# A hybrid two-layer backbone whose instruction order is set by the framework's timeline model

## The chip, the cores and the metric

The kernel runs on one core of a Trainium2 chip. The metric is the device time of one execution in microseconds (us), as a median of several executions. The core has five engines that run their own instruction streams in program order: TensorE (PE, matrix products), VectorE (DVE), ScalarE (ACT), GpSimd (POOL) and SyncE (SP, whose instructions here only issue DMA transfers). An engine that meets an instruction whose input isn't there yet waits, and everything behind that instruction on the same engine waits with it.

## What is computed

The reference is a backbone of two layers over 1024 latent tokens and 256 context tokens, 1024 wide, in float32.

```python
def hybrid_layer(x_lat, x_ctx, mod_lat, mod_ctx, p, layer_idx, need_ctx):
    sh1, sc1, g1, sh2, sc2, g2 = jnp.split(mod_lat[:, None, :], 6, axis=-1)
    ...
    hl = rms_norm(x_lat, p['norm1_g']) * (1.0 + sc1) + sh1
    ...
    zl = split_cols(hl @ p['w_in'])
    ...
    s5 = s5_mixer(zc[0], zl[0], p, need_ctx)
    ml = mlstm_mixer(zc[1:6], zl[1:6], p, need_ctx)
    da = diff_attention_mixer(zc[6:9], zl[6:9], p, layer_idx, need_ctx)
    gl = gla_mixer(zc[9:14], zl[9:14], p, need_ctx)
    mix_l = jnp.concatenate([s5[1], ml[1], da[1], gl[1]], axis=-1) @ p['w_out']
    x_lat = x_lat + g1 * mix_l
    hl2 = rms_norm(x_lat, p['norm2_g']) * (1.0 + sc2) + sh2
    x_lat = x_lat + g2 * sq_relu_mlp(hl2, p['mlp_w1'], p['mlp_w2'])
```

The context tokens go through the same layer with their own modulation, except that the second layer needs no context output (`need_ctx` is false there). The four mixers are a state space model (S5), an mLSTM, differential attention and gated linear attention (GLA).

## The kernel before

**Arithmetic.** Every large product is done as three products of split operands (a high and a low part of each side), at the helper's lines L1124, L1125 and L1126. So three matmuls stand for one. A weight block comes from memory into a tile `raw` (L1112, on SP's queue, three buffers that the modulation's weights `adaw`, L1159, share), ACT casts it to `whi` (L1115), and DVE forms the rest `wlo` (L1116).

**Stages of a layer.** The input projection writes PSUM tiles `zp`; ACT copies each to `zst` (L1261), and a DMA stores it. The S5 mixer runs beside it: PE multiplies the input blocks (`s5pv`, L350), ACT, POOL and DVE run the state recurrence (`s5V`, `s5W`, `s5Z`, `s5X`), and PE reads the state out (`s5py`, L308 and L313). `da_prep` rotates the attention's queries and keys and stores them (`da_st`, L447). GLA follows (`glpl` L1014, `glpo` L1059 and L1064, and the mean square for its norm, `glms` L1072). Then comes differential attention: scores `daps` (L486), their copy with a running maximum on DVE (`das`, L487), exponentials on ACT (L498), the combination of the two maps on DVE (L506), transposes `dapt` (L527), the product with the values `dapo` (L518), and a norm (`dams` L552). The mLSTM runs beside attention: a convolution and an activation prepare its queries and keys on DVE and ACT (tiles `mlcy`, `mlqT`, `mlkT`, L722 to L734), then PE transposes (`mlpt` L756) and updates states (`mlpu` L788). The first half of the output projection (`wop`, needing only S5 and GLA) is also put beside attention; its second half follows. Then come a norm (`np`, `npm`) and the MLP (`m1p`, `m2p`). In layer 0's MLP the S5 tables of layer 1 (`s5_prep`) and the modulation (`ada`) are computed beside the products.

**What sets the order.** The Python code issues the instructions in one sequence. Generators are interleaved by helpers; three such places matter here:

```python
        beside(both(s5_mix(...), 2, dap, 1), rest, 1300)
        ...
        beside(gla, rest, 1400)
        ...
        beside((1 for _ in both(da, 1, ml, 0.25)), po, 0.12)
```

Here `rest` are the steps of the input projection, `po` those of the first half of the output projection, and the number says how much filler goes beside one step. On top of this sequence the tile framework has a scheduler: it keeps a model of the machine, goes through the instructions, and sets for each engine the order in which they are written to that engine's stream. So the order on an engine need not be that of the code. Data dependencies and the reuse of buffers are kept by semaphores in any order.

## Time and profile before

| | |
|---|---|
| median of 3 executions | 3724.48 us (3724.34 to 3726.04) |
| the profiled execution | 3719.97 us, span 3718.2 us |
| PE busy | 3435.5 us, 92% of the span |
| PE's weight loads (PEld) busy | 2725.4 us, 73% |
| DVE busy | 2228.8 us, 60% |
| ACT busy | 1309.4 us, 35% |
| POOL busy | 450.7 us, 12% |
| mean granted TensorE clock | 0.952 |

The span is that of one profiled execution, from its first instruction to its last. Busy time counts an engine's own instructions; successive matmuls overlap in PE's pipeline, so a busy PE isn't one that works at its peak. The granted clock is a share of the full 2.4 GHz; the rows know two levels, 0.5 (1.2 GHz) and 1.0 (2.4 GHz), and a value between them in a stretch is a mean.

### The profile page before, as it was taken

The page shows a single profiled execution, that of the slowest core. Times are in us where ns is not written, and L with a number is a line of the kernel's source. Part 1 is how long each engine was busy: PE and PEld are TensorE (multiplying, and loading weights), DVE is VectorE, ACT ScalarE, POOL GpSimd, SP SyncE. Part 2 cuts the span into 40 slices and gives each one's busy share as a digit, 9 for nine tenths or more (in the row PEclk, how much of TensorE's full clock was granted, in tenths as well). Part 3 has the DMA queues.
Part 4 walks back from the last instruction along what each step waited for, and adds up shares of the span by engine and source line. Part 5 has one row for each costly group of instructions (what it writes and reads, how often), then busy time and mean ns, then how long its engine had stood idle before and what let it go on. Part 6 is the DMA issues. An engine that isn't in the chain of part 4 may idle for free. (4 is left out here: it accounts for less than half of the span.)

```text
span 3718.2 us, 53487 instructions
## 1 busy us (share of the span) xinstructions
PE 3435.5 (92%) x20338; PEld 2725.4 (73%) x20338; DVE 2228.8 (60%) x5455; ACT 1309.4 (35%) x2457; POOL 450.7 (12%) x520
## 2 busy tenths in 40 slices
PE   6989998798889999999999798988889899999998
PEld 3867767576658888888888476867677578888885
DVE  9654685877659855455544637486788543333334
ACT  4223434766542121212121522435676431222222
POOL 2121221222100000000000123120222000000000
PEclk8979999898899999999999998999889899999999
DMA  5665324655461221222111265314653611111112
GB/s 216 230 205 154 129 77 133 214 183 166 141 208 57 90 82 69 81 74 86 61 39 42 102 201 161 120 57 143 213 167 104 205 46 51 46 51 46 52 47 78
DMA packets 233959, 430.23 MB, mean 116 GB/s; under 512 B 47415, under 2 KB 135911, under 8 KB 233447
## 3 DMA queue, kind: packets, MB, share of 16 engines
q1 hardware_dynamic: 192806, 381.03, 31.2%
q10 hardware_dynamic: 35520, 30.52, 2.6%
q0 software_dynamic: 5376, 15.28, 1.2%
q8 instruction: 160, 2.62, 0.3%
q14 instruction: 97, 0.79, 0.1%
HBM read 316.88 MB, written 109.86 MB: 115 GB/s over the span
## 5 line engine op out<-in xcount | busy, mean ns | idle before, releaser
L1562 DVE SCALAR_TENSOR_TENSOR X<-m2p,mods,X 128x256 f32<-128x256 f32 (+1 forms) x512 | 345.7, 683 | 345.1 <-PE m2p L1126 344.6
L1115 ACT CAST whi<-raw 128x1024 fp32r<-128x1024 f32 x182 | 191.1, 1050 | 919.8 <-PE m2p L1125 638.0
L1124 PE MATMUL m2p<-hidhi,whi 128*128 128x512 f32 (+1 forms) x1280 | 473.8, 372 | 3.5 <-DVE X L1562 2.8
L1124 PE MATMUL m1p<-h2hi,whi 128*128 128x512 f32 (+1 forms) x1280 | 474.3, 371 | 0.2 <-ACT h2hi L1209 0.2
L1125 PE MATMUL m1p<-h2lo,whi 128*128 128x512 f32 (+1 forms) x1280 | 473.6, 370 | 0.0
L1125 PE MATMUL m2p<-hidlo,whi 128*128 128x512 f32 (+1 forms) x1280 | 473.1, 370 | 0.0
L1126 PE MATMUL m2p<-hidhi,wlo 128*128 128x512 f32 (+1 forms) x1280 | 472.2, 370 | 0.8 <-DVE wlo L1116 0.8
L1126 PE MATMUL m1p<-h2hi,wlo 128*128 128x512 f32 (+1 forms) x1280 | 472.6, 370 | 0.0
L1116 DVE TENSOR_TENSOR wlo<-raw,whi 128x1024 fp32r<-128x1024 f32 x182 | 224.7, 1235 | 313.2 <-ACT whi L1115 301.2
L1124 PEld LDWEIGHTS m2p<-hidhi,whi 128*128 128x128 f32 x1280 | 241.6, 189 | 59.6 <-issue 8.6
L1124 PEld LDWEIGHTS m1p<-h2hi,whi 128*128 128x128 f32 x1280 | 243.1, 190 | 46.2 <-ACT whi L1115 4.2
L1126 PEld LDWEIGHTS m2p<-hidhi,wlo 128*128 128x128 f32 x1280 | 241.2, 188 | 46.4 <-issue 3.4
L1125 PEld LDWEIGHTS m1p<-h2lo,whi 128*128 128x128 f32 x1280 | 243.4, 190 | 40.8 <-DVE h2lo L1210 0.8
L1126 PEld LDWEIGHTS m1p<-h2hi,wlo 128*128 128x128 f32 x1280 | 243.2, 190 | 40.3 <-issue 0.4
L1125 PEld LDWEIGHTS m2p<-hidlo,whi 128*128 128x128 f32 x1280 | 241.6, 189 | 42.0 <-issue 2.2
L1124 PE MATMUL zp<-hhi,whi 128*128 128x512 f32 (+1 forms) x664 | 254.2, 383 | 11.6 <-ACT zst L1237 9.6
L487 DVE TENSOR_SCALAR_CACHE_REDUCE das<-daps 128x512 f32<-128x512 f32 (+1 forms) x400 | 226.0, 589 | 58.4 <-PE daps L486 55.0
L1125 PE MATMUL zp<-hlo,whi 128*128 128x512 f32 (+1 forms) x664 | 251.2, 378 | 5.6 <-DVE hlo L1205 5.2
L1126 PE MATMUL zp<-hhi,wlo 128*128 128x512 f32 (+1 forms) x664 | 249.5, 376 | 0.0
L1576 DVE TENSOR_TENSOR rl<-rl,m1p 128x256 f32<-128x256 f32 (+1 forms) x160 | 100.8, 631 | 177.1 <-ACT rl L1575 177.1
L498 ACT ACTIVATE das<-das,danm 128x1280 f32<-128x1280 f32 x128 | 174.3, 1362 | 42.7 <-DVE danm L496 42.3
L486 PE MATMUL daps<-daqk,daqk 128*128 128x512 f32 (+1 forms) x400 | 153.3, 447 | 38.0 <-DVE das L487 36.6
(460 smaller groups left out, 6671.3 us busy)
## 6 DMA issues: line engine op xcount, KB each, us to landing
raw<-w SPq DMA_DIRECT2D x136, 512.0 KB
adaw<-ada_w SPq DMA_DIRECT2D x96, 512.0 KB
whl<-wsp SPq DMA_DIRECT2D x80, 512.0 KB
wsp<-whl SPq DMA_DIRECT2D x32, 512.0 KB
raw<-wz SPq DMA_DIRECT2D x30, 512.0 KB
daqk<-da_st SPq DMA_DIRECT2D x24, 640.0 KB
mlE<-ml_rows SPq DMA_DIRECT2D x16, 640.0 KB
xn<-xo SPq DMA_DIRECT2D x72, 128.0 KB
```

The lines of the kernel that those rows point to most:

```text
L486: pe.matmul(p[:, 0:b - a], Q[m][:, 128 * qt:128 * qt + 128], K[m][:, a:b], start=True, stop=True)
L487: v.tensor_scalar(s[:, a:b], p[:, 0:b - a], -1.0, None, op0=ALU.mult, op1=ALU.min, accum_out=pm[:, i:i + 1])
L498: act.activation(s[:, :k1], s[:, :k1], AF.Exp, bias=nm[:, 0:1], scale=-1.0, accum_out=sm[m])
L1115: nc.scalar.copy(hi, raw)
L1116: nc.vector.tensor_tensor(lo, raw, hi.bitcast(F32), op=ALU.subtract)
L1124: pe.matmul(out, ah, bh, start=i == 0, stop=False)
L1125: pe.matmul(out, ah, bl, start=False, stop=False)
L1126: pe.matmul(out, al, bh, start=False, stop=i == n - 1)
L1562: nc.vector.scalar_tensor_tensor(X[b][:, m], p[:, :n], mod(l, 5, s)[:, m:m + 1], X[b][:, m], op0=ALU.mult, op1=ALU.add)
L1576: nc.vector.tensor_tensor(rl[:, :n], rl[:, :n], p[:, :n], op=ALU.mult)
```

## The change

```diff
-    with tile.TileContext(nc) as tc:
+    with tile.TileContext(nc, schedule_with_timeline_sim=True) as tc:
         tile_hybrid_backbone(tc, io, out)
```

The framework's scheduler now goes by a timeline model of the machine in place of its default model. The instructions are the same in kind and number, with the same tiles and pools; what differs is their order on each engine, and with it the semaphore waits that go along (3,160 semaphore instructions where there were 3,118).

**S5 and the projection in layer 0, on PE.** In the rows of an engine's order a number behind a tile's name is its buffer, and xN stands for N equal instructions in a row. Before, where the first S5 groups of layer 0 begin, PE had:

```order
L1126 MATMUL zp<-hhi_377,wlo 128x512
L350 MATMUL s5pv<-U,s5mi 64x160 x16
L308 MATMUL s5py<-U,s5toep 128x160
L313 MATMUL s5py<-s5X,s5mo 128x160 x4
L308 MATMUL s5py<-U,s5toep 128x160
L313 MATMUL s5py<-s5X,s5mo 128x160 x4
L350 MATMUL s5pv<-U,s5mi 64x160 x8
L1162 MATMUL adap<-adaw,cst 32x512 x4
L1169 MATMUL adap_2272<-selada,adar 128x2 x4
```

Now it has first

```order
L350 MATMUL s5pv<-U,s5mi 64x160 x8
L308 MATMUL s5py<-U,s5toep 128x160 x2
L350 MATMUL s5pv<-U,s5mi 64x160 x8
L313 MATMUL s5py<-s5X,s5mo 128x160 x4
L1124 MATMUL zp<-hhi_379,whi 128x512
L1125 MATMUL zp<-hlo_380,whi 128x512
L1126 MATMUL zp<-hhi_379,wlo 128x512
```

and, behind 16 more rows of `zp`,

```order
L313 MATMUL s5py<-s5X,s5mo 128x160 x4
L1125 MATMUL zp<-hlo_380,whi 128x512
L1126 MATMUL zp<-hhi_379,wlo 128x512
L1124 MATMUL zp<-hhi_379,whi 128x512
L1125 MATMUL zp<-hlo_380,whi 128x512
L1126 MATMUL zp<-hhi_379,wlo 128x512
L350 MATMUL s5pv<-U,s5mi 64x160 x8
L1169 MATMUL adap_2272<-selada,adar 128x2 x4
L1124 MATMUL zp<-hhi_375,whi 128x256
L1125 MATMUL zp<-hlo_376,whi 128x256
L308 MATMUL s5py<-U,s5toep 128x160
L1126 MATMUL zp<-hhi_375,wlo 128x256
```

Products of the projection now stand between the groups of S5, where before 47 instructions of S5 and the modulation stood next to each other. On SP the load of projection weights (`raw`, L1112) that stood behind the first four rows of S5's table loads (`s5tbl`, L346), and the load of the value weights `wn` that stood behind eight such rows, now stand ahead of the first.

**The end of GLA and the start of attention in layer 0, on PE.** Before, the last product of GLA stood 267 instructions ahead of these rows, with `zp` alone between:

```order
L1126 MATMUL zp<-whi,hlo_380 128x256
L672 MATMUL mlpt<-ident,ig 128x104
L673 MATMUL mlpt<-ident,mlbb 128x104
L681 MATMUL mlpt<-mlam,mle 128x40
L756 MATMUL mlpt<-ident,mlkT 128x128 x10
L788 MATMUL mlpu<-mlvx,mlkw 64x65
L486 MATMUL daps<-daqk_6076,daqk_6078 128x256
L486 MATMUL daps<-daqk_6072,daqk_6074 128x256
L486 MATMUL daps<-daqk_6076,daqk_6078 128x256 x2
L486 MATMUL daps<-daqk_6072,daqk_6074 128x256
L486 MATMUL daps<-daqk_6076,daqk_6078 128x512 x2
L486 MATMUL daps<-daqk_6072,daqk_6074 128x512
L1124 MATMUL wop<-mh,whl 128x256
```

Now the products of GLA are spread among those of the projection, 12 to 37 `zp` between two groups, and the end is this, with `zp` ahead of it:

```order
L1126 MATMUL zp<-whi,hlo_380 128x256
L1072 MATMUL glms<-glsq,bones 128x512
L1014 MATMUL glpl<-glqd_4176,glkt 64x256 x4
L1014 MATMUL glpl<-glqd_4177,glkt 64x256 x4
L1014 MATMUL glpl<-glqd_4176,glkt 64x256 x4
L486 MATMUL daps<-daqk_6076,daqk_6078 128x256
L1014 MATMUL glpl<-glqd_4177,glkt 64x256 x4
L1014 MATMUL glpl<-glqd_4176,glk 64x256 x4
L1059 MATMUL glpo<-glqd_4177,glS_3586 64x2x64 x4
L1059 MATMUL glpo<-glqd_4176,glS_3587 64x2x64 x4
L1064 MATMUL glpo<-glA,glv 64x64 x8
L1059 MATMUL glpo<-glqd_4177,glS_3586 64x2x64 x4
```

followed, behind one more row of `glpo`, by

```order
L1064 MATMUL glpo<-glA,glv 64x64 x8
L1072 MATMUL glms<-glsq,bones 128x256 x2
L486 MATMUL daps<-daqk_6076,daqk_6078 128x256
L486 MATMUL daps<-daqk_6072,daqk_6074 128x256
L486 MATMUL daps<-daqk_6076,daqk_6078 128x256
L486 MATMUL daps<-daqk_6072,daqk_6074 128x256
L486 MATMUL daps<-daqk_6076,daqk_6078 128x512 x2
L486 MATMUL daps<-daqk_6072,daqk_6074 128x256
L486 MATMUL daps<-daqk_6072,daqk_6074 128x512
L1124 MATMUL wop<-mh,whl 128x256
L1125 MATMUL wop<-ml,whl 128x256
```

The last block of GLA (the context tokens') now comes behind the projection with nothing beside it, and attention starts at once behind it. The mLSTM's transposes `mlpt`, which stood ahead of the first scores, come among the attention's rows, 47 to 214 instructions behind the first eight scores in a row, and the first `mlpu` stands 242 instructions behind them, where it stood just ahead. On DVE the mLSTM's convolution (L723, L734) stood ahead of the first `das`, and now stands 52 to 140 rows behind it. In layer 1, which has no context block, GLA is spread in the same way, 19 `zp` stand between its last `glpo` and its last `glms`, and the mLSTM's preparation stays ahead of the first `das`.

**Elsewhere.** In attention the `wop` rows come in whole groups of 12, and in layer 0 they reach to the last 40 instructions ahead of the last `dams`, where before the last 200 had none. Behind the last `dams` the `wop` of the second half follow at once in both. In the MLPs `m1p` and `m2p` keep their order; layer 1's S5 tables, which were spread to the end of layer 0's MLP, are now done by its middle.

## Rows read from the trace of the kernel before

**Rows 1.** The page's first part: busy time, share of the span, instructions.

```profile
PE 3435.5 (92%) x20338; PEld 2725.4 (73%) x20338; DVE 2228.8 (60%) x5455; ACT 1309.4 (35%) x2457; POOL 450.7 (12%) x520
```

**Rows 2.** Engines' busy time, TensorE clock, DMA by stretch: four long stretches.

```profile
core 0: us, PE busy (x) PEld busy (x) DVE busy (x) ACT busy (x) POOL busy (x), PEclk, DMA share, GB/s
68.00:656.00 588.00, 530.49 (x3770) 419.94 (x3767) 378.57 (x835) 216.07 (x417) 120.58 (x153) 0.92 0.49 154
656.00:995.00 339.00, 299.25 (x2290) 235.59 (x2290) 271.39 (x919) 220.05 (x496) 78.54 (x76) 0.92 0.53 172
2155.00:2597.00 442.00, 394.75 (x2847) 320.45 (x2845) 278.44 (x512) 161.61 (x291) 102.04 (x112) 0.95 0.42 131
2597.00:2931.00 334.00, 290.71 (x2121) 225.51 (x2120) 257.88 (x811) 213.21 (x445) 74.04 (x62) 0.88 0.53 170
```

**Rows 3.** The same view, by stage.

```profile
214.00:387.00 173.00, 157.38 (x883) 122.95 (x878) 95.98 (x216) 52.34 (x114) 41.28 (x61) 0.85 0.56 178
387.00:450.00 63.00, 58.97 (x692) 48.80 (x691) 44.91 (x84) 29.14 (x54) 14.58 (x8) 1.00 0.33 116
450.00:565.00 115.00, 102.70 (x759) 69.74 (x758) 95.36 (x163) 46.84 (x85) 31.60 (x24) 0.97 0.21 71
565.00:605.00 40.00, 37.11 (x321) 32.35 (x321) 20.61 (x46) 12.28 (x30) 7.14 (x8) 1.00 0.21 69
605.00:638.00 33.00, 32.01 (x263) 31.41 (x262) 19.77 (x45) 17.86 (x24) 2.74 (x18) 1.00 0.63 151
638.00:656.00 18.00, 3.59 (x19) 2.63 (x18) 13.92 (x18) 15.20 (x29) 0.00 (x0) 0.58 0.97 323
995.00:1118.00 123.00, 98.51 (x443) 62.64 (x443) 61.16 (x101) 50.05 (x90) 5.07 (x7) 0.92 0.60 202
1118.00:2054.00 936.00, 932.74 (x5039) 780.07 (x5038) 548.22 (x1491) 182.78 (x318) 35.65 (x69) 0.99 0.20 68
2155.00:2350.00 195.00, 172.22 (x1002) 140.99 (x1001) 105.49 (x217) 50.37 (x105) 55.47 (x65) 0.93 0.55 167
2350.00:2413.00 63.00, 61.85 (x673) 51.67 (x672) 37.20 (x67) 30.79 (x55) 9.60 (x6) 1.00 0.31 109
2413.00:2530.00 117.00, 103.84 (x717) 75.73 (x718) 99.51 (x152) 44.78 (x76) 31.80 (x22) 0.96 0.17 58
2530.00:2597.00 67.00, 56.85 (x462) 52.07 (x458) 36.24 (x78) 35.68 (x56) 5.16 (x19) 0.92 0.56 171
```

**Rows 4.** PE's waits, S5 stage of layer 0, 212 to 390 us.

```profile
PE s5py L313 <- DVE s5X L374: 4.3, 1, 4.3
PE s5py L308 <- DVE s5Y L316: 3.6, 4, 1.8
```

**Rows 5.** Loads of raw weights on SP's queue, 200 to 300 us.

```profile
L1112 SPq DMA_DIRECT2D raw<-wn x2: 424/427/430, 282.3 to 283.4; - x2
L1112 SPq DMA_DIRECT2D raw<-wz x1: 431/431/431, 233.8 to 233.8; - x1
```

**Rows 6.** PE's waits, GLA stage of layer 0, 390 to 605 us.

```profile
PE glpl L1014 <- DVE glqd L1007: 7.9, 10, 2.3
PE glms L1072 <- ACT glsq L1070: 4.0, 3, 2.0
```

**Rows 7.** PE's waits, first attention head, layer 0, 636:757.

```profile
PE mlpu L788 <- issue: 11.0, 1, 11.0
PE daps L486 <- DVE das L487: 9.4, 8, 6.4
```

**Rows 8.** PE's waits, S5 stage of layer 1, 2155:2350.

```profile
PE s5py L313 <- DVE s5X L374: 14.2, 4, 7.0
```

**Rows 9.** The same view, instructions on tile mlcy alone: DVE, ACT, clock, DMA.

```profile
605.00:656.00 51.00, 21.90 (x24) 5.82 (x4) 0.85 0.75 212
```

**Rows 10.** PE's waits between attention and MLP, layer 0, 995:1118.

```profile
PE wop L1124 <- ACT mh L1444: 9.0, 3, 7.4
```

## The prediction

> **What bounds the kernel now.** I read the page's busy shares first. PE is busy for 92% of the span and DVE for 60% [rows 1], so PE sets the time, but a busy PE includes matmuls at half clock and matmuls that overlap. I therefore read busy time and clock by stretch, and for each stretch took what PE loses: wall time less busy time times granted clock. That is the time in which PE either had nothing to do or did it at 1.2 GHz. A better order can give back this time and no other, since the products themselves stay.
>
> The layer 0 MLP shows a stretch without such loss: 936 us of wall, 932.74 busy at 0.99, so 936 - 923 = 13 us lost [rows 3]. The reader should see that a quarter of the span lies there, and that next to nothing is to be had in it; layer 1's MLP is the same work for fewer tokens. The four mixer stretches are different [rows 2]: 588 - 530.49 x 0.92 = 100 us lost in the projection with S5 and GLA of layer 0, 339 - 275 = 64 in its attention, 442 - 375 = 67 in layer 1's projection with S5 and GLA, 334 - 256 = 78 in layer 1's attention. The change works on these 309 us.
>
> By stage [rows 3] the loss of the projection parts is this. S5 of layer 0 (214 to 387 us): 173 - 157.38 x 0.85 = 39. GLA of layer 0 (387 to 605): 4 + 15.4 + 2.9 = 22. The projection's tail (605 to 638) loses 1, so the products alone fill PE. The step into attention (638 to 656) loses 18 - 3.59 x 0.58 = 16. S5 of layer 1 (2155 to 2350): 195 - 160 = 35. GLA of layer 1 and the step into its attention (2350 to 2597): 1 + 17.3 + 14.7 = 33.
>
> The waits tell why. In S5, PE stands at the read-out for DVE's states, 4.3 us and 3.6 us in layer 0 [rows 4] and 14.2 us in layer 1 [rows 8], and nothing of the projection stands in between on PE to fill this. Loads are one reason: between 200 and 300 us SP issued only three loads of projection weights, the first at 233.8 us and the others at 282.3 to 283.4 us [rows 5]. The named waits make only a fifth of the 39 us; the rest is the clock, 157.38 x 0.15 = 24 us, which fell while PE had only small products with pauses. In GLA, PE stands for `glqd` ten times, 7.9 us, and for the norm's squares, 4.0 us [rows 6]. So both stages have the form of short stalls in a chain over DVE and ACT, with 33 us of pure projection work [rows 3] left behind them in which nothing stalls.
>
> **The change, part by part.** The sum is made against the profiled execution's own time, 3719.97 us, which is 4.5 us under the median of 3724.48.
>
> *S5 with the projection, both layers.* The order now puts `zp` products between the S5 groups. At the first place of layer 0 the run of S5 and modulation without a `zp` shrinks from 47 instructions to 22, and the later groups have one to nineteen `zp` between them. Nothing is added: the products come out of the tail, where they were not covering anything. 25 of 47 is 53%, and later groups are covered better, so I take 60% of the loss: 0.6 x 39 = 23 in layer 0 and 0.6 x 35 = 21 in layer 1. The bounds: only the waits named in the rows, 8 and 14, or the whole, 39 and 35.
>
> *GLA with the projection, both layers.* With 12 to 37 `zp` between two groups, the waits for `glqd` have cover. DVE is the next engine: it worked 95.36 of 115 us in the dense part (450 to 565), but over 387 to 638 it has 44.91 + 95.36 + 20.61 + 19.77 = 181 us of 251 [rows 3], so spreading GLA over the tail leaves DVE room. The same 60% gives 0.6 x 22 = 13 and 0.6 x 33 = 20. The bounds: 8 and 8 (the named `glqd` waits, for layer 1 taken as in layer 0), or 22 and 33.
>
> *The step into attention, layer 0.* Gone is the stall at the first `mlpu`, 11.0 us, and the longest at `daps`, 6.4 us [rows 7]; with the clock this was 16 us plus 6, or 22. In its place stands the context block of GLA with no `zp` beside it. The trace has no such uncovered block; the nearest rows are the longest waits of a covered one, 2.3 us for a group of `glpl` and 2.0 for `glms` [rows 6]. Five groups and two norms make 5 x 2.3 + 2 x 2 = 15.5 us, and the first `wop` must wait for its operand `mh`, whose longest wait elsewhere was 7.4 us [rows 10]: 23 us. So the one stall takes the place of the other and I put 0, with bounds of -10 (the chain overlaps the first scores) and +20 (both stalls stay, as `mlpu` only moves).
>
> *The mLSTM's preparation, layer 0.* It lay under the projection's tail and the step behind it; now it stands behind the first `das`. On DVE the convolution's tile alone takes 21.9 us, on ACT 5.8 [rows 9]. In attention DVE has 271.39 of 339 us [rows 2], 68 us free, so it may cost nothing; if DVE sets attention's pace it costs 21.9. DVE is four fifths full there, and long instructions in front of a `das` hold up `daps` on PE: I take +10. Queued behind them on DVE are the score copies, and for these PE's scores wait, with `wop` groups between as cover. The Trainium skill (SBUF — State Buffer, section "SBUF: two separate sides") says that a DVE operation with two SBUF inputs and a GpSimd operation that reads SBUF shut each other out for whole instructions. The convolution has two such inputs; POOL was busy for 2.74 us of the tail but for 78.54 of 339 us in attention, so by this rule an estimate is 0.23 x 21.9 = 5 us more, and the sum would be 5 us higher. No run here shows it yet, and the sum goes without it.
>
> *Attention's fillers.* Whole groups of `wop` up to the end give the transposes cover, but spread what there is; the second half of the output projection must still wait for the last head. The stretch behind attention already loses 123 - 98.51 x 0.92 = 32 us, of which 9.0 are waits for `mh` [rows 10, 3]. With no `wop` left over I put +4 for each layer's end, and nothing for the cover in the middle. Bounds: -10 and +15 in all for each layer.
>
> *The MLPs.* Their products keep their order, and the S5 tables of layer 1 run on DVE and ACT, which are less than 60% busy there. Cost 0, bounds -5 and +10 against the 13 us lost there.
>
> The sum: -23 - 21 - 13 - 20 + 0 + 10 + 8 + 0 = -59 us. 3720 - 59 = 3661 us for an execution like the profiled one, and 3665 us with the 4.5 us up to the median.
>
> **Rivals.**
>
> *A. The queue of SP turns S5 over (slower).* The loads of projection weights now stand ahead of S5's tables on SP. They have three buffers, shared with the modulation's weights, so a load waits for the cast of the third block before, that cast for a `whi`, and that for `zp` on PE; S5's table and matrix loads stand behind it. For it: SP's loads of weights were already 49 us apart [rows 5]. Against it: `zp` run earlier now and free the buffers earlier. If half of the 32 S5 steps of both layers then show a wait for states of 4.3 us [rows 4], this is 16 x 4.3 = 69 us, the 44 us of S5 are not won, and the sum is +69 - 33 + 18 = +54: 3778 us at the median. It decides from 15 + 7 = 22 us of such waits on, 0.7 us for each step.
>
> *B. Attention gives it back (about no change).* If DVE sets the pace in layer 0's attention, its work there becomes 271.39 + 21.9 + 13.92 from the step before = 307 us, and at its old share of 0.80 this takes 384 us, behind a GLA tail of 23: 407 against 18 + 339 = 357 before, so +50. With +8 for the ends and 77 won, this is -19; if the projection stages give only 60 it is -2, 3722 us. For it: DVE is the fullest engine beside PE there. Against it: 68 us of DVE's time are free, and PE's 64 us lost there show that neither engine binds alone.
>
> *C. More is won.* If the clock stays at 2.4 GHz through S5 and every chain is covered, the whole loss of 39 + 22 + 35 + 33 = 129 us comes back, less 18: 3720 - 111 + 4.5 = 3613 us. For it: in the tail with dense products the clock was 1.00. Against it: the S5 chain cannot start before its input is projected, and runs of 22 instructions without cover stay.
>
> *D. Only the named waits go.* 8 + 14 + 8 + 8 = 38 won, less 18: 3704 us at the median.
>
> **How the numbers follow.** My forecast has a chance of 0.43, with its own range of 3630 to 3695 us; D has 0.10, C 0.10, B 0.14, A 0.23. A measurement of this kernel tells about 0.2% (7 us) from no change. Forecast, C and D are faster, and B where the projection gives its 77, for which I put 0.05 of its 0.14: 0.68. Another 0.07 of B is the same. The last 0.02 of B and A are slower: 0.25. The range leaves out the far half of A and the far part of C: 3605 to 3765 us.
>
> **What would show it.** In the new profile the S5 stage of layer 0 should end some 20 us earlier, with a granted clock above 0.9, and SP should issue weights there more evenly. GLA should show waits for `glqd` of under 4 us in all, except in an uncovered last block of 15 to 25 us. Attention of layer 0 should take about 10 us more than its 339, with DVE above 84%. The MLPs should last as before to within 1%. I am wrong if S5's stage is no shorter (then look at SP's waits ahead of table loads: A), or if layer 0's attention is over 40 us longer (B), or if the MLPs move, which none of these steps holds.

## The result and the profile after

The change makes the kernel slower. Its median is 3761.05 us (3758.97 to 3762.14, four executions) against 3724.41 us (3714.79 to 3726.04, four), a ratio of 1.0103 with a 95% interval of 1.0085 to 1.0121, or 37 us: small, but clear of no change. The prediction was 3665 us, faster.

The first part of the page of the changed kernel, in answer to [rows 1]:

```profile
PE 3479.6 (93%) x20338; PEld 2727.3 (73%) x20338; DVE 2240.9 (60%) x5455; ACT 1309.9 (35%) x2457; POOL 467.4 (12%) x520
```

The counts are those of before. PE is busier than before, and the kernel is longer all the same. So busy PE is not the thing to look at; the stages have to be followed one by one. The view of one tile gives for each group of instructions its count, its shortest, median and longest duration in ns, and the starts of the first and the last. In layer 0 of the kernel before, for the last projection products, GLA's norm, the last step of the mLSTM's preparation, and the norms of the attention heads:

```profile
L1126 PE MATMUL zp<-whi,hlo x320: 274/283/561, 299.2 to 638.3; 128*128 128x256 f32 x160
L1072 PE MATMUL glms<-glsq,bones x12: 379/592/697, 501.2 to 604.4; 128*128 128x512 f32 x8, 128*128 128x256 f32 x4
L734 DVE SCALAR_TENSOR_TENSOR mlqT<-mlcy,mlqT x4: 421/822/1222, 640.7 to 652.9; 128x256 f32<-128x256 f32 x2, 128x1024 f32<-128x1024 f32 x2
L552 PE MATMUL dams<-dasq,bones x16: 275/586/736, 679.9 to 1009.4; 128*128 128x128 f32 x8, 128*128 128x512 f32 x8
```

The same view of the changed kernel:

```profile
L1126 PE MATMUL zp<-whi,hlo x320: 277/283/415, 273.9 to 589.4; 128*128 128x256 f32 x160
L1072 PE MATMUL glms<-glsq,bones x12: 379/591/796, 512.0 to 623.6; 128*128 128x512 f32 x8, 128*128 128x256 f32 x4
L734 DVE SCALAR_TENSOR_TENSOR mlqT<-mlcy,mlqT x4: 406/810/3942, 680.7 to 696.9; 128x256 f32<-128x256 f32 x2, 128x1024 f32<-128x1024 f32 x2
L552 PE MATMUL dams<-dasq,bones x16: 415/586/1222, 652.5 to 1023.2; 128*128 128x128 f32 x8, 128*128 128x512 f32 x8
```

The projection ends 49 us earlier (638.3 to 589.4). But GLA's last norm is 19 us later, the mLSTM's preparation 44 us later, and the last head's norm 14 us later: the 49 us are gone by the end of attention, and 14 more. From starts like these every later table of stages is made. "Step" is the time from the last `zp` to the second `dams` pair of layer 0 and to the first of layer 1, that is from the end of the projection to the end of the first heads; "rest" is from there to the last `dams`; MLP 0 is from the first to the last `m1p`; "projection 1" is from layer 0's last `m2p` to layer 1's last `zp`.

| us | last zp, layer 0 | step 0 | rest 0 | MLP 0 | projection 1 | step 1 | rest 1 |
|---|---|---|---|---|---|---|---|
| before | 638 | 118 | 253 | 934 | 475 | 113 | 218 |
| after | 589 | 165 | 268 | 959 | 441 | 141 | 215 |
| difference | -49 | +47 | +15 | +25 | -34 | +28 | -3 |

The differences add up to +29; the rest of the 37 us lies in the short pieces between: behind the heads of layer 1, 77 us become 83, and behind the last `m1p` of layer 0, 57 become 60.

Where attention's step grew is seen in the busy times by stretch (columns as in [rows 2]). First the kernel before: step and rest of layer 0, step of layer 1:

```profile
638.00:756.00 118.00, 85.88 (x632) 65.47 (x631) 97.23 (x288) 80.44 (x178) 24.43 (x20) 0.84 0.70 229
756.00:1009.00 253.00, 225.46 (x1753) 179.53 (x1754) 192.83 (x661) 161.61 (x362) 56.66 (x58) 0.92 0.49 160
2582.00:2695.00 113.00, 90.03 (x606) 68.55 (x605) 89.22 (x277) 77.13 (x158) 26.70 (x18) 0.83 0.69 228
```

The two steps of the changed kernel, and ahead of them a stretch of its GLA stage:

```profile
445.00:512.00 67.00, 67.00 (x523) 49.43 (x524) 54.28 (x84) 27.89 (x48) 18.41 (x13) 1.00 0.28 91
589.00:754.00 165.00, 119.28 (x734) 85.25 (x733) 129.88 (x359) 101.71 (x216) 41.17 (x43) 0.73 0.61 192
2588.00:2730.00 142.00, 101.65 (x617) 74.40 (x616) 118.38 (x328) 96.22 (x183) 33.40 (x35) 0.76 0.64 199
```

DVE has 33 us more to do in the first step and 29 us more in the second: GLA's last blocks and the first half of the mLSTM's preparation, which stood ahead of the projection's end, now stand behind it. Its share of the time hardly moves (0.82 and 0.79 before, 0.79 and 0.83 after), and the clock of PE falls from 0.84 to 0.73 and from 0.83 to 0.76. With two levels, 0.73 over 165 us means 89 us at 1.2 GHz, where 0.84 over 118 us meant 38; how much of the longer step is due to that, and how much of it only follows from PE's pauses, no run separates. In 445 to 512 us, from the first `glpl` of GLA to its first norm, PE is busy for 67.00 of 67 us at full clock: projection products fill every gap, and GLA's first norm comes 11 us later than before (512.0 against 501.2).

PE's waits in GLA of layer 0, 374 to 631 us (total us, times, longest), in answer to [rows 6]:

```profile
PE glpl L1014 <- DVE glkt L1000: 9.0, 4, 4.4
PE glms L1072 <- ACT glsq L1070: 7.8, 3, 7.1
PE glpo L1059 <- DVE glqd L1051: 2.4, 2, 1.5
```

The ten waits of `glpl` for `glqd` are gone. What is left is one wait of 7.1 us at the last norm and waits of up to 4.4 us for `glkt`, all but 1.4 us of them in the tail where no projection product is left.

The MLP of layer 0 has no such story, since PE waits only 3.8 us at its start and 0.5 us later. Its stretches, before and after:

```profile
1115.00:2049.00 934.00, 930.74 (x5029) 777.85 (x5028) 544.78 (x1487) 180.77 (x316) 35.65 (x69) 0.99 0.20 68
```

```profile
1128.00:2087.00 959.00, 954.71 (x5031) 777.72 (x5030) 541.55 (x1490) 180.11 (x317) 35.68 (x69) 1.00 0.20 66
```

The same work at the same clock, 24 us more busy. The instruction groups by form name the place: the modulation's products on PE in this stretch, before and after (count, total us, mean ns, idle before):

```profile
L1162 PE MATMUL adap<-adaw,cst 128*32 128x512 f32 x176 | 24.5, 605 | 0.0
```

```profile
L1162 PE MATMUL adap<-adaw,cst 128*32 128x512 f32 x176 | 41.1, 605 | 0.0
```

The same 176 records with the same mean of 605 ns cover 24.5 us before and 41.1 us after. So before they lay over each other, and now they do less. The timeline of PE shows it (start, us, instruction; each product of this kind leaves two records, so x8 is four products). Before, four products together:

```profile
1304.36 0.39 PE L1126 MATMUL m2p<-hidhi,wlo 128*128 128x512 f32 x1
1304.68 1.06 PE L1162 MATMUL adap<-adaw,cst 128*32 128x512 f32 x8
1305.68 0.39 PE L1124 MATMUL m1p<-h2hi,whi 128*128 128x256 f32 x1
```

After, one product alone, and a second one alone 2.56 us later:

```profile
1522.80 0.39 PE L1126 MATMUL m2p<-hidhi,wlo 128*128 128x512 f32 x1
1523.12 1.04 PE L1162 MATMUL adap<-adaw,cst 128*32 128x512 f32 x2
1524.10 0.50 PE L1124 MATMUL m2p<-hidhi,whi 128*128 128x512 f32 x1
...
1525.68 1.04 PE L1162 MATMUL adap<-adaw,cst 128*32 128x512 f32 x2
1526.66 0.39 PE L1124 MATMUL m2p<-hidhi,whi 128*128 128x256 f32 x1
```

From its start to the next product of the MLP four products take 1.00 us, and one takes 0.98 us. Each of the four writes its own 32 columns (`tile_position=(0, 32 * j)`), and they run side by side. The new order breaks the groups of four into twos and ones, and each piece costs the whole price. Counted from each record's start to the next one's, these products take 22.9 us in 23 pieces before and 38.4 us in 39 pieces after: 16 of the 25 us. Another 5 us are the products of the norm (`np`, `npm`) and the wait at the start, and 3 us are the S5 tables, which also stand in more pieces.

### The profile page after: what moved, and what is told of

It is laid out like the page before. It is cut to its first block, busy times and chain, and to the rows that moved or that the text cites. A ratio compares the mean times of both kernels' runs of the same rounds, so it can differ in the third digit from the quotient of the medians.

```text
span 3757.2 us, 53529 instructions
## 1 busy us (share of the span) xinstructions
PE 3479.6 (93%) x20338; PEld 2727.3 (73%) x20338; DVE 2240.9 (60%) x5455; ACT 1309.9 (35%) x2457; POOL 467.4 (12%) x520
## 5 line engine op out<-in xcount | busy, mean ns | idle before, releaser
L486 PE MATMUL daps<-daqk,daqk 128*128 128x512 f32 (+1 forms) x400 | 161.0, 466 | 52.3 <-DVE das L487 43.2
L1124 PE MATMUL wop<-mh,whl 128*128 128x256 f32 (+1 forms) x448 | 161.2, 363 | 33.1 <-ACT mh L1444 22.0
## 6 DMA issues: line engine op xcount, KB each, us to landing
raw<-w SPq DMA_DIRECT2D x136, 512.0 KB
adaw<-ada_w SPq DMA_DIRECT2D x96, 512.0 KB
whl<-wsp SPq DMA_DIRECT2D x80, 512.0 KB
wsp<-whl SPq DMA_DIRECT2D x32, 512.0 KB
raw<-wz SPq DMA_DIRECT2D x30, 512.0 KB
```

Of the source, the lines that this page charges most:

```text
L486: pe.matmul(p[:, 0:b - a], Q[m][:, 128 * qt:128 * qt + 128], K[m][:, a:b], start=True, stop=True)
L1124: pe.matmul(out, ah, bh, start=i == 0, stop=False)
```

## The experiments

All kernels but one are the kernel before with one more line: it orders the instructions of each engine by a written-out table, by edges that hold the order of issue only. Data dependencies, tiles and semaphores' rules stay. Each table is spliced from the order of before and the order of the change. In e6 to e11, e13 and e15 a variant of this line can also leave an engine free in a stretch.

```diff
+def pin(tc, packed):
+    ...
+    for i in ids:
+        x = ins["I-%d" % i]
+        if x.engine in last:
+            tc.add_manual_dep(x, last[x.engine], mybir.DependencyInfo(mybir.DependencyClass.NoSync, mybir.DependencyReason.DATA), reason="pin")
+        last[x.engine] = x.name
...
         tile_hybrid_backbone(tc, io, out)
+        pin(tc, ORDER)
```

The stages of the runs, made as in the table above, with the median and the ratio (of means) to the kernel before on the same chip:

| | last zp 0 | step 0 | rest 0 | MLP 0 | projection 1 | step 1 | rest 1 | median, ratio [95%] |
|---|---|---|---|---|---|---|---|---|
| e1 | 595 | 163 | 268 | 937 | 449 | 143 | 216 | 3750.80, 1.0079 [1.0049, 1.0110] |
| e14 (e1 again) | 593 | 160 | 267 | 935 | 451 | 140 | 212 | 3742.12, 1.0067 [1.0041, 1.0093] |
| e5 (the change) | 599 | 160 | 268 | 959 | 450 | 140 | 215 | 3768.57, 1.0121 [1.0103, 1.0140] |
| e6 | 639 | 120 | 260 | 953 | 472 | 111 | 211 | 3741.09, 1.0051 [1.0034, 1.0068] |
| e2 | 636 | 122 | 260 | 931 | 481 | 112 | 211 | 3723.81, 0.9997 [0.9979, 1.0014] |
| e3 | 596 | 183 | 258 | 936 | 450 | 159 | 218 | 3774.92, 1.0134 [1.0111, 1.0157] |
| e4 | 639 | 138 | 272 | 935 | 475 | 131 | 216 | 3775.94, 1.0139 [1.0114, 1.0163] |
| e7 | 639 | 130 | 324 | 936 | 479 | 122 | 257 | 3871.22, 1.0402 [1.0379, 1.0425] |
| e8 | 640 | 136 | 278 | 933 | 474 | 124 | 243 | 3796.50, 1.0198 [1.0179, 1.0218] |
| e9 | 639 | 136 | 309 | 936 | 475 | 131 | 268 | 3859.77, 1.0348 [1.0320, 1.0376] |
| e11 | 640 | 120 | 253 | 1080 | 477 | 112 | 211 | 3872.74, 1.0385 [1.0363, 1.0407] |
| e12 | 662 | 107 | 259 | 935 | 503 | 106 | 211 | 3757.89, 1.0079 [1.0054, 1.0104] |
| e13 | 606 | 161 | 276 | 934 | 468 | 142 | 217 | 3775.75, 1.0151 [1.0133, 1.0170] |
| e15 | 619 | 159 | 268 | 935 | 458 | 142 | 216 | 3771.71, 1.0122 [1.0088, 1.0156] |

**e5: the control.** It holds the changed order whole, on every engine, as a written-out table.

```diff
         tile_hybrid_backbone(tc, io, out)
+        pin(tc, ORDER)
```

> The changed kernel once more, its whole order written out and issued under the default scheduler: the same instructions in the same order on every engine. It tells how far a second chip or day moves the result beside which the other runs stand. All theories: 3755 to 3775 us; the MLP of layer 0 again 959 us, attention of layer 0 (end of projection to last norm) 430 to 435 us.

It repeats the change, and shows how far a stage moves between chips with no change at all: 10 us in the first projection (599 against 589), 9 in the second, 5 in step 0. Differences of that size in these stages are not read below; the MLP's column moves less, 931 to 937 us in the eleven runs that leave its order as before. The whole change is 46 us over the kernel before on this chip, where it was 37.

**e1: the changed order with layer 0's MLP as before.**

A piece of PE's order there, in the changed kernel and in e1 (the other engines follow before's order too, from the first `m1p` to the last `m2p` of the layer):

```diff
+L1162 MATMUL adap<-adaw,cst 32x512 x4
...
-L1162 MATMUL adap<-adaw,cst 32x512 x2
...
-L1162 MATMUL adap<-adaw,cst 32x512
...
-L1162 MATMUL adap<-adaw,cst 32x512
```

> The changed order everywhere except in layer 0's MLP, whose instructions on every engine are issued in the order of before. Theory P (pieces): the changed order breaks PE's side work in that MLP (modulation and S5 tables) into 100 visits where there were 63, a visit costs PE about 1.2 us however small it is, and this is the 28 us by which that MLP is longer in the trace. Then 28 us come back: 3733 us (3726 to 3740). Rival: the MLP is longer because of what it inherits (clock, weights' buffers, a late start), and stays so: 3755 to 3761 us.

The MLP took 937 us, as before, and lost the 22 us of the change. The whole came down less than expected, to 24 us over the kernel before: the projections took 6 to 8 us longer than in the changed kernel, as in the control.

**e6: the kernel before, with groups of four modulation products in that MLP broken in two.** A piece of PE's order, before and in e6, where nothing else moves:

```diff
-L1162 MATMUL adap<-adaw,cst 32x512 x4
+L1162 MATMUL adap<-adaw,cst 32x512 x2
 L1124 MATMUL m2p<-hidhi,whi 128x256
 ...
 L1124 MATMUL m2p<-hidhi,whi 128x256
+L1162 MATMUL adap<-adaw,cst 32x512 x2
```

> The order of before with one edit: in layer 0's MLP, 21 of the groups of four modulation products (L1162) are broken into two and two, with four products of the MLP between the halves. No instruction is added. Theory P: a visit of PE to the modulation costs about 1.25 us whether it has two products or four, so 21 further visits cost 26 us, all in that MLP: 960 us there in place of 934, 3750 us in all. Rival: two products cost half of four: no change, 3724 us.

The MLP of e1, and that of e6, by stretch:

```profile
1134.00:2070.50 936.50, 932.40 (x5028) 779.47 (x5027) 544.44 (x1486) 180.83 (x317) 35.62 (x69) 0.99 0.20 68
```

```profile
1127.00:2080.00 953.00, 951.84 (x5027) 778.04 (x5028) 544.49 (x1486) 181.09 (x316) 35.73 (x69) 1.00 0.20 66
```

21 more pieces cost 953 - 934 = 19 us, 0.9 us each (26 us were expected), in the kernel before with nothing else touched. With e1, which takes the stage's whole new order away from the change, the MLP's 25 us are shown from both sides: they come from the order inside the stage, and the broken groups, at the price that e6 measures, are the larger part of them.

**e2 and e3: how much of the projection's new order.** e2 takes the changed order from the start of the projection to the first `glpt`, that is for S5 alone; e3 takes it to the last `zp`, so for GLA too. Both do so in both layers, and leave the rest as before.

```diff
         tile_hybrid_backbone(tc, io, out)
+        pin(tc, ORDER)
```

> The order of before everywhere except from the start of each layer's input projection to the first GLA transpose, where the changed order is issued. Theory: the time won beside S5 is real and independent of what follows; S5 ends 13 us earlier in layer 0 and 18 us earlier against its start in layer 1, more of the projection is done by then, and nothing is given back: 3685 to 3700 us. Rival: the projection products used beside S5 are missing beside GLA, and the gain is given back there: 3715 to 3727 us.

> The order of before everywhere except from the start of each layer's input projection to its last product, where the changed order is issued, GLA's spread included. Theory: 49 and 35 us are won there as in the trace of the changed kernel; in layer 0 the last block of GLA (30 us of products with waits) and the mLSTM's preparation (33 us of work on VectorE) then lie bare ahead of the scores, so about 55 us are given back: 3685 to 3705 us. Rival: all is given back, since attention can't start before the mLSTM is prepared in this order: 3724 to 3760 us.

GLA's norm and the end of the mLSTM's preparation in e2, and then in e3:

```profile
L734 DVE SCALAR_TENSOR_TENSOR mlqT<-mlcy,mlqT x4: 420/822/1219, 638.1 to 650.2; 128x256 f32<-128x256 f32 x2, 128x1024 f32<-128x1024 f32 x2
L1072 PE MATMUL glms<-glsq,bones x12: 379/592/697, 498.0 to 601.2; 128*128 128x512 f32 x8, 128*128 128x256 f32 x4
```

```profile
L734 DVE SCALAR_TENSOR_TENSOR mlqT<-mlcy,mlqT x4: 418/822/1219, 662.7 to 674.8; 128x256 f32<-128x256 f32 x2, 128x1024 f32<-128x1024 f32 x2
L1072 PE MATMUL glms<-glsq,bones x12: 379/591/793, 518.7 to 627.9; 128*128 128x512 f32 x8, 128*128 128x256 f32 x4
```

Putting projection products between the S5 groups wins nothing that lasts: 3723.81 against 3726.62 us. S5's last product starts at 313.0 us against 318.2, and GLA ends at 601 us against 604. In e3 the last `zp` comes 42 us earlier, and GLA 24 and the preparation 22 us later; the steps into attention grow by 65 and 46 us, and the kernel is 48 us slower. Between the two kernels stands only the new order of GLA with the rest of the projection: 51 us. That is more than either expectation allowed, and more than the change itself costs, which has the preparation of the mLSTM in another place.

**e4, e7, e8: attention alone.** e4 takes the changed order in both attention stages and nothing else; e7 does so for PE alone and leaves the other engines free, e8 for DVE, ACT, POOL and SP alone.

```diff
         tile_hybrid_backbone(tc, io, out)
+        pin(tc, ORDER)
```

> The order of before everywhere except from the first scores of each layer to the first product of its MLP, where the changed order is issued; GLA's tail and the mLSTM's preparation stay ahead of the scores as before. Theory A: attention's own changed order costs time (more, smaller pieces of the mLSTM and of the products with the values, clock lower), 15 us for each layer: 3745 to 3760 us. Rival: attention is longer in the changed kernel only because of what is carried into it, GLA's last block and the mLSTM's preparation; its own order costs nothing: 3718 to 3730 us.

> The order of before, except that in both attention stages (first scores to the first product of the MLP) PE issues in the changed order; the other engines are left to the default scheduler there. Theory A1: it is PE's order that makes attention longer (mLSTM late, fillers in whole groups): +39 and +16 us as in the run with all engines in the changed order, 3770 to 3780 us. Rival A2: it is the order on DVE and ACT that does it: 3724 to 3735 us.

> The order of before, except that in both attention stages DVE, ACT, POOL and SP issue in the changed order; PE is left to the default scheduler there. Theory A1 (PE's order is the cause): 3724 to 3735 us. Rival A2 (the order on DVE and ACT is the cause, above all when score copies stand behind long combinations): 3765 to 3780 us. If both this run and the one with PE's order alone are slow, either order carries the same sequence of work.

Attention's own order costs 20 + 19 us in layer 0 and 18 - 2 in layer 1, more than the 15 us for each layer that were expected. PE's waits hardly account for it: those for the scores' copies (`daps <- das`) come to 28.3 us in 23 pieces in layer 0, and to 23.5 us in 18 pieces before. PE is busy for longer with the same products, 94.66 + 249.79 = 344 us in step and rest, where it was 85.88 + 225.46 = 311:

```profile
638.80:776.80 138.00, 94.66 (x622) 71.14 (x621) 93.99 (x277) 81.89 (x176) 25.16 (x18) 0.75 0.60 201
776.80:1048.70 271.90, 249.79 (x1780) 198.77 (x1778) 204.98 (x677) 166.78 (x368) 59.37 (x60) 0.91 0.47 153
```

A part of that has the same sign as in the MLP. The products with the values (`dapo`, which write alternate halves of 64 columns) and one product of the mLSTM (`mlpn`, whose inputs alternate between halves of 64 rows), in layer 0 before:

```profile
L518 PE MATMUL dapo<-dawT,davt 128*64 128x128 f32 x672 | 63.3, 289 | 1.3 <-ACT dawT L528 1.3
L826 PE MATMUL mlpn<-mlC,mlab 64*128 64x65 f32 x160 | 16.9, 297 | 1.6 <-POOL mlab L795 1.6
```

And in e4:

```profile
L518 PE MATMUL dapo<-dawT,davt 128*64 128x128 f32 x672 | 71.3, 290 | 0.7 <-ACT dawT L528 0.7
L826 PE MATMUL mlpn<-mlC,mlab 64*128 64x65 f32 x160 | 23.9, 296 | 0.0
```

The counts are the same and the means within 1 ns, and they cover 15 us more, in 114 and 27 groups where there were 90 and 21. No run isolates these pieces. The lower clock is another part: 0.75 against 0.84 in the step. Neither half gives the price of the whole: PE's order alone costs 148 us, the other engines' 74. Here a mixed order is worse than either of the two whole ones, and outside what either theory expected, so the halves don't say which engine's order is at fault.

**e9: the kernel before, with the mLSTM's instructions placed in attention as in the changed order.**

A piece of PE's order in the first head, before and in e9:

```diff
 L486 MATMUL daps<-daqk_6072,daqk_6074 128x512 x2
 L486 MATMUL daps<-daqk_6072,daqk_6074 128x256
-L486 MATMUL daps<-daqk_6076,daqk_6078 128x512
-L788 MATMUL mlpu<-mlvx,mlkw 64x65 x4
-L486 MATMUL daps<-daqk_6076,daqk_6078 128x512
+L486 MATMUL daps<-daqk_6076,daqk_6078 128x512 x2
```

> The order of before, except that in both attention stages the mLSTM's instructions stand where the changed order has them against PE's attention instructions; attention and the fillers keep their own order of before. Theory M: the mLSTM's place is what makes the changed attention longer: most of the +28 and +25 us of the run with the whole changed order, 3765 to 3780 us. Rival: it is the order within attention and its fillers; the mLSTM's place costs nothing: 3720 to 3735 us.

132 us slower, between two and three times e4, which holds the same placement. It overshoots what it should explain, so it is a second mixed order that is worse than both, and settles nothing about the mLSTM.

**e11: fewer pieces than before.** If pieces cost, groups of eight modulation products should win; 17 pieces fewer in the MLP of layer 0.

```diff
-L1162 MATMUL adap<-adaw,cst 32x512 x4
+L1162 MATMUL adap<-adaw,cst 32x512 x8
```

> The order of before with PE's side work in layer 0's MLP gathered into 17 fewer visits: the two groups of four modulation products of a chunk together, and the two parts of an S5 table step together. If a visit has a fixed cost beside its products (a group of four takes 1.09 us beyond the MLP product that follows, of which 0.52 us are its own), 10 merged pairs give 10 x 0.56 = 5.6 us and 7 merged table steps about 2 us: 3715 us against 3723. If only broken groups of four cost, nothing: 3723 us.

The MLP took 1080 us. PE's waits there, which the kernel before does not have:

```profile
PE adap L1162 <- DMA adaw<-ada_w: 32.4, 10, 3.4
PE m2p L1124 <- DVE rl L1576: 31.0, 10, 3.3
PE adap L1169 <- ACT adar L1166: 20.9, 10, 5.8
```

Eight products in a row need four weight tiles, and these come through three buffers that the MLP's own weights share; the largest of these waits is for their loads. All of PE's waits in the stage come to 98 us, and its clock falls to 0.93 from 0.99; whether the expected gain of some 8 us is in there can't be seen.

**e12 and e13: GLA earlier.** e12 changes the code and not the order table: less projection work is put beside each step of GLA. e13 is e1 with GLA of both layers, from its preparation to its first norm, in before's order.

```diff
-        beside(gla, rest, 1400)
+        beside(gla, rest, 1000)
```

A piece of DVE's order, in e1 and in e13:

```diff
-L967 SCALAR_TENSOR_TENSOR glS_3586<-glS_3586,gldec,glpu 128x64 x16
-L1116 TENSOR_TENSOR wlo<-raw,whi 128x1024
-L967 SCALAR_TENSOR_TENSOR glS_3586<-glS_3586,gldec,glpu 128x64 x3
+L967 SCALAR_TENSOR_TENSOR glS_3586<-glS_3586,gldec,glpu 128x64 x19
```

> The kernel before with the rate of projection products beside GLA at 1000 in place of 1400, under the default scheduler: fewer products of the projection ahead of GLA's steps (1272 ahead of the first GLA product in layer 0 in place of 1310; the changed order has 1416), more behind. Theory C (chain): attention starts when the chain S5, GLA, mLSTM preparation is through on VectorE, not when the projection ends; then GLA ends some 4 to 8 us earlier and the time is the same or lower, 3712 to 3726 us, though the projection ends later. Rival (PE is the bound, products held back are only late): GLA stage no shorter in sum, 3728 to 3745 us.

> The changed order with layer 0's MLP as before, as in the first experiment (3751 us), and in addition GLA from its preparation to its first norm in the order of before, in both layers: 1310 and 1186 projection products stand ahead of the first GLA product in place of 1416 and 1312. Theory C: those 106 and 126 products ahead are where the time won beside S5 is lost, since they stand on PE in front of members of the chain that attention waits for; the preparation took 39 us before and 59 us in the changed order. Then GLA ends 15 to 20 us earlier in each layer and 25 to 35 us come back in all: 3716 to 3726 us. Rival: PE's projection work must be done anyway and what is put behind costs as much there: 3745 to 3760 us.

> The first experiment once more, as the control of the run beside it on the same chip: the changed order with layer 0's MLP in the order of before. All theories: 3745 to 3755 us, GLA's end in layer 0 at 625 to 632 us.

The norms of GLA in e12 and in e13:

```profile
L1072 PE MATMUL glms<-glsq,bones x12: 379/592/1222, 503.4 to 608.2; 128*128 128x512 f32 x8, 128*128 128x256 f32 x4
```

```profile
L1072 PE MATMUL glms<-glsq,bones x12: 379/591/796, 490.9 to 640.2; 128*128 128x512 f32 x8, 128*128 128x256 f32 x4
```

Less filler did not make GLA end earlier (608 against 604 us), and the projection ended 24 and 28 us later; the steps became only 11 and 7 us shorter, and the kernel 31 us slower, past both ranges. In e13 the first norm comes 25 us earlier than in e14 (490.9 against 515.8) and the last one 15 us later (640.2 against 624.7). The kernel is 56 us slower than before, where e14 is 22. So the theory that the changed GLA ends late because its beginning stands behind too many projection products finds no support: a head start at its front does not reach its end, in this splice of two orders.

**e15: cover for GLA's tail.** e1, with the last 192 projection products of layer 0 put between the groups of GLA's last block, and the first scores behind it.

```diff
 L1126 MATMUL zp<-whi,hlo 128x256
+L1014 MATMUL glpl<-glqd,glk 64x256 x8
+L1014 MATMUL glpl<-glqd,glkt 64x256 x4
 ...
-L1126 MATMUL zp<-whi,hlo 128x256
```

> The changed order with layer 0's MLP as before (3751 and 3742 us in two runs), with one more edit in layer 0: the last 192 projection products (the mLSTM's output gate, needed late) are taken out from between GLA's earlier groups and put between the groups of its last block, which stood behind the projection with nothing beside it; attention's first scores follow. Theory T (tail): that bare block costs about 20 us of PE's time and clock between the end of the projection and the end of GLA; now GLA ends with the projection, 10 to 15 us earlier, and 10 to 20 us come back: 3725 to 3738 us. Rival D (DVE): GLA's last block comes through no earlier, since it goes through DVE and ACT, and the time does not move: 3742 to 3755 us.

GLA's last norm came at 627.4 us, no earlier than in e14 (624.7), with the first of these waits still in front of it and the second behind it:

```profile
PE glms L1072 <- ACT glsq L1070: 7.5, 1, 7.5
PE daps L486 <- DMA daqk<-da_st: 6.4, 1, 6.4
```

So the tail's end does not hang on PE being without work, and covering it wins nothing: what is left in front of it is a wait for ACT. The kernel is 47 us slower than before, where e1 and e14 are 24 and 22, so both theories missed. Step 0 remained at 159 us, though the projection ended 26 us later than in e14 and DVE had 113 us left to do behind it against 129. So DVE's work behind the projection's end, which goes with the step's length in before and after, is not by itself what sets that length either. What did move with the end of the step is the mLSTM's preparation, which now starts its last `mlqT` at 719.9 us:

```profile
L734 DVE SCALAR_TENSOR_TENSOR mlqT<-mlcy,mlqT x4: 406/810/3933, 703.7 to 719.9; 128x256 f32<-128x256 f32 x2, 128x1024 f32<-128x1024 f32 x2
```

In e14 that is 697.4 us, and the second `dams` pair follows it by 57 us here and by 55 us there. It starts 92 us behind GLA's last norm here and 73 there; why, no run shows.

## Why the prediction was wrong

**S5 and GLA with the projection: the sum was right by luck, and the account was wrong.** The terms were -23 and -13 in layer 0, -21 and -20 in layer 1. The projections took 49 and 34 us less, 83 against 77 in sum. But with S5's part alone (e2) the last `zp` comes 2 us earlier and projection 1 is no shorter, where 44 us were forecast; with GLA's part as well (e3) the projections are 42 and 25 us shorter. Of the signs named in advance some came: the `glqd` waits of `glpl` are gone, S5's clock is 0.94 (214 to 374 us), and an uncovered tail is left, with a clock of 0.73 in the step from 589 us on. Others did not: S5's last product starts 7 us earlier and not some 20, SP's three loads of projection weights in 200 to 300 us are no more even (209 to 284 us), and DVE's share from the projection's end to the last norm of layer 0 is 0.77 and not above 0.84. And this gain was not time. The step that failed is the method, "in which PE either had nothing to do or did it at 1.2 GHz. A better order can give back this time": it credits PE's recovered loss as if PE's end released what comes next. What attention's first heads follow is GLA's end and the mLSTM's preparation on DVE and ACT, and these ended 19 and 44 us later. The starts of the runs show it. In the kernel before, e2, e3 and e6, where attention keeps its old order, the last `zp` comes between 596 and 639 us. The last `mlqT` starts 47 to 49 us behind GLA's last norm in all four, and the second `dams` pair 103 to 108 us behind that, while the distance from the last `zp` goes from 118 to 183 us. In e12, with the last `zp` at 662 us, it is 49 and 112. In the six runs with the changed order there, the pair follows the last `mlqT` by 55 to 57 us. S5's part of the gain is worth nothing (0.9997), and GLA's part has the projection end early and the kernel 51 us slower.

**The step into attention, put at 0 (bounds -10 and +20), was +47 and +28.** The prediction saw that the stall at the first `mlpu` would be replaced by GLA's bare tail, and priced that tail by PE's waits, 15.5 us, with 7.4 for the first `wop`. The tail's waits came out at about that: 9.0 + 7.8 + 2.4 = 19 us over the whole of GLA. What was left out is that 33 us of DVE's work come along, and that GLA ends behind the projection in layer 1 too, where DVE's work in the step grew by 29 us; there the sum had no such term, and counted the step's loss as something to win.

**The mLSTM's preparation, +10.** It moved as foreseen, and its work on DVE did not grow much. The price of the place can't be told apart: e9, which was to isolate it, overshot. The sentence on the shared port can now be read from the trace. In the changed kernel, DVE's last two `mlqT` steps at 696 us (one row; the second, 1024 columns wide, is the long one) and an `mlE` product:

```profile
695.86 0.67 DVE L487 TENSOR_SCALAR_CACHE_REDUCE das<-daps 128x512 f32<-128x512 f32 x1
...
696.52 4.27 DVE L734 SCALAR_TENSOR_TENSOR mlqT<-mlcy,mlqT 128x256 f32<-128x256 f32 x2
700.72 4.17 DVE L765 TENSOR_TENSOR mlE<-mlE,mlcm 128x1280 f32<-128x1280 f32 x1
```

POOL at the same time:

```profile
696.75 2.96 POOL L765 TENSOR_TENSOR mlE<-mlE,mlcm 128x1280 f32<-128x1280 f32 x1 [10.72 <-DMA mlE<-ml_rows]
700.08 3.46 POOL L765 TENSOR_TENSOR mlE<-mlE,mlcm 128x1280 f32<-128x1280 f32 x1 [0.36 <-DMA mlE<-ml_rows]
```

And the same `mlqT` steps and an `mlE` product of the same form in the kernel before, while POOL stood idle for the 33.64 us up to 657.29:

```profile
647.14 1.49 DVE L765 TENSOR_TENSOR mlE<-mlE,mlcm 128x1280 f32<-128x1280 f32 x1
...
652.52 1.56 DVE L734 SCALAR_TENSOR_TENSOR mlqT<-mlcy,mlqT 128x256 f32<-128x256 f32 x2 [1.24 <-ACT mlqT L732]
```

```profile
657.29 1.42 POOL L867 TENSOR_TENSOR mlog<-mlog,mlgn 128x256 f32<-128x256 f32 x2 [33.64 <-ACT mlog L601]
```

Each of the two rows took 2.7 us longer beside a POOL product of some 3 us. The rule of the Trainium skill (SBUF — State Buffer, section "SBUF: two separate sides"), that a DVE operation with two SBUF inputs and a GpSimd operation that reads SBUF take turns for whole instructions, agrees with this. The estimate for the convolution was 5 us; these rows show 2.7 us on it, and as much on another instruction. It is a small part of 47 us.

**Rival B came nearest.** It took DVE's work as moved, at DVE's old share of 0.80, and came to +50 for layer 0's attention. Measured, from the projection's end to the last norm, are +62. Its mechanism fits before and after, where DVE's share in the step hardly changed; e15 shows that it is not that simple. It had nothing for layer 1, where the step grew by 28 us, and so ended at about no change. It had a chance of 0.14.

**Attention's fillers, +8.** The short stretch behind attention moved by -1 and +6. The order inside attention cost more: by e4 some 39 and 16 us where it is changed alone, with 15 us in layer 0 on products that cover more time in more pieces. In the whole change it is 15 and -3 in the rests, so the two parts do not add: +48 for e3 and +49 for e4 by themselves, and +22 for both together (e14, 3742.12 - 3719.63). The heads of the changed order begin beside GLA's tail, and in e3 and e4 they cannot.

**The MLPs, "Cost 0, bounds -5 and +10".** This was wrong, and the cause is shown. MLP 0 lasted 25 us more, some 16 of them by the broken groups of the modulation. "Their products keep their order" holds for `m1p` and `m2p`; the prediction did not look at the side work between them. The loss of PE there was 13 us, and so it seemed that there was nothing to win; that does not bound what can be lost. The reason given for the method, "since the products themselves stay", fails here as well: the same 176 records cover 41.1 us in place of 24.5.

**Rivals A, C and D** did not come. For A, PE's longest waits in S5 of layer 0 are 5.2 us for weights of the modulation and 5.1 us for S5's input, and those for states come to 3.0 and 1.6 us; A began at 15 + 7.

With MLP 0 at 25 us and its end at 3, the rest of the change is 9 us in the first comparison, 18 in e5, and 24 and 22 us in e1 and e14. What stays open is which piece of the new order of GLA and of attention costs how much. The splices that would have told it don't: e7, e8, e9 and e13 are slower than both of the orders that they were made of, and e3 and e4, each with a part of the change, are no faster than the whole. Of all versions run, none beat the kernel before: e2 equals it.

## What to carry to other kernels

Before you credit an engine's recovered idle time, name the chain that releases the next stage, and see whether its last link moves: here PE was full and at full clock beside GLA's first products, most of its waits there were gone, and the chain over DVE ended later. Where an order changes, look at the small work between the large products too: products that run side by side must stay together, and a stage with nothing to win can still lose. A splice of two orders is a third order: where it is slower than both, as four were here, it says little of either.

## What the runs showed of the hardware

Four matmuls on separate groups of 32 columns take as long as one, if they stand together: 1.00 us from their start to the next product, and 0.98 us for one alone. Nothing in the clock (1.00) or in the busy share (954.71 of 959 us) betrays the loss when they are pulled apart, and no wait for it is seen; only the time that the same count of records covers does (24.5 and 41.1 us).
